# Remainders and 128x1024 products from GpSimd to VectorE in a two-layer decoder trunk, with the loop's weight rows placed anew

## The chip, the cores and the metric

The kernel runs on one core of a Trainium2 chip. The metric is the time of one execution on the device in microseconds (us), the median of several runs. The core's engines are TensorE (matmul; PE in the profile, and PEld for its weight loads), VectorE (DVE), ScalarE (ACT), GpSimd (POOL) and SyncE (SP, which issues the DMAs here).

## The reference

The program computes two layers on x of 1024 tokens by 1024 columns, in float32. Layer 0 is RWKV-7 time mixing, layer 1 differential attention; each ends with a gated embedding, and a root-mean-square norm closes the whole. Layer 0, which most of the change is in, is cut here to what is computed:

```python
dx = token_shift(h) - h                       # h = rms_norm(x)
r, k, v, gate = (h + dx * mu[g]) @ w_in[:, g] # g = 0..3
decay, a = f(h + dx * mu[4]), f2(h + dx * mu[5])
# per head of 64, over the 1024 tokens:
state = state * w_t - (state @ kk_t) * b_t + v_t * k_t
y_t = state @ r_t
y = (y - mean) * rsqrt(var + eps) * ln_w + ln_b
y = y + sum(r * k * r_k) * v                  # bonus
h = x + (y * silu(gate)) @ w_out
h = h + sigmoid(rms_norm(h) @ pe_w_gate) * (p @ pe_w_proj)
```

Layer 1 projects h to q, k, v and a gate for 8 heads, takes softmax twice for each head, subtracts one from the other times lambda, norms, gates, multiplies by w_out, and ends with the same gated embedding.

## The kernel before

**Products in three parts.** A float32 operand is used as two: a high part of reduced precision, which ACT makes by a copy, and the remainder, the operand less its high part. `split` (line 86) issues both; the remainder runs on the engine it is given, on POOL when none is given. A product is then three matmuls (`mm3`, line 90): high by high, high by remainder, remainder by high. So each weight row (128x1024) and each tile of activations needs a remainder before its second matmul.

**Stages in the order of the program.** The norm and the transposes of x; the projections k, r, v and gate, one after another; a loop over 16 chunks of 64 tokens; the gated embedding of layer 0; attention, head by head; its output product and the last gate.

- `make_xm` (line 251) makes the input of projection g for 128 columns and 512 tokens: a scaled copy, a multiply-add on DVE, and a split. `make_half` does eight of them; the halves of v and of gate are made while r and v still run. `wload` (267) loads and splits a weight row: names w1, w0 for k and r, wv for v, w3 for gate.
- Beside v and gate run the inverses of 32x32 blocks (`inv_diag`, 565): sums row by row on DVE (tiles tm and tb), with small products on TensorE before and behind (pb, pg, po).
- In the loop, chunk c has pieces of the chunk itself (`chain_x`, `chain_u`, `chain_s`), of the next chunk's preparation (`stage1`: decayed, turn, mh, pr, bonus), and of the 128-token tile two chunks back (`d1_pieces`: load, norm, squares, bonus_v in the even chunk; sums, roots, scaled, added, turn in the odd one). The tile before that one is multiplied by w_out: m0 (first 512 columns) in the even chunk and m1 in the odd one, in four pieces of two weight rows, which `more` places between the chains. In the first four chunks `more` places products of layer 1's embedding in their stead. `wo_row` (965) splits the rows of w_out, one by one, in chunks 1 to 4.
- `gate_row` (761) makes a gate's weight row, scaled by the norm's vector: with an engine given, ACT scales the row, ACT copies it, and the engine subtracts; with none, ACT writes the scaled high part at once and DVE makes the remainder in one multiply-subtract (`wrow`, 743).

**Order.** In the loop, from line 1091 to 1206, each engine keeps the order in which the program issues its instructions. Elsewhere the framework's planner orders each engine's instructions by its own simulated times; the listing gives only the dependences and priorities. Every engine works through its own queue in order. All DMAs named here are issued on SP's queue, but for the gate's store on ACT's.

Of the kernel before, what the change touches and what calls it, by code (L numbers as in the profile page):

```python
# [16 lines left out]
ALU = mybir.AluOpType  # L17
# [4 lines left out]
P = 128  # L22
D = 1024
SEQ = 1024
KT = D // P
NT = SEQ // P
L = 64
# [10 lines left out]
def trunk(ctx: ExitStack, tc: tile.TileContext, A, out):  # L38
# [47 lines left out]
    def split(hi, lo, src, lo_eng=None):  # L86
        S.activation(hi, src, AF.Copy)
        (lo_eng or G).tensor_tensor(out=lo, in0=src, in1=hi.bitcast(F32), op=ALU.subtract)
# [132 lines left out]
    with NB("ab") as ab, NP("psab") as pp:  # L221
# [29 lines left out]
        def make_xm(g, kt, hf):  # L251
            h, lo = xslot(f"xm{g}_{kt}_{hf}")
            t = ab.tile([P, 512], F32, tag="xmt", name=f"xmt{g}_{kt}_{hf}", bufs=3)
            hc = hT[:, kt, hf * 512 + 1:hf * 512 + 513]
            if kt % 2 and g != 3:
                V.tensor_scalar(out=t, in0=hc, scalar1=cA[:, g, kt:kt + 1], scalar2=None, op0=ALU.mult)
            else:
                S.activation(t, hc, AF.Copy, scale=cA[:, g, kt:kt + 1])
            V.scalar_tensor_tensor(out=t, in0=hT[:, kt, half(hf)], scalar=cB[:, g, kt:kt + 1], in1=t,
                                   op0=ALU.mult, op1=ALU.add)  # L260
            split(h, lo, t, V if kt % (2 if g == 1 else 3 if g != 3 else 8) == 1 else G)
            return h, lo

        def make_half(g, hf):
# [2 lines left out]
        def wload(nm, src):  # L267
            r = wraw(nm + "r")
            nc.sync.dma_start(out=r, in_=src)
            h, lo = wpair(nm)  # L270
            split(h, lo, r)
            return h, lo

        def dense_T(g, src, xm, ev, nxt, tick=lambda: None):
# [581 lines left out]
    with NB("d") as d, NP("psco") as pp:  # L856
# [114 lines left out]
        def d1_pieces(i):  # L971

            w = D1[i]
            rows = slice(i * P, (i + 1) * P)
            y = w["y"]

            def load():
                w["v"] = dt_("vn", f"vn{i}")
                nc.sync.dma_start(out=w["v"], in_=v_d[rows, :])
                w["sg"] = kview(dt_("sg", f"sg{i}"))  # L980
                nc.sync.dma_start(out=w["sg"], in_=sg_d[:, :, rows].rearrange("j p t -> p j t"))
                w["x"] = dt_("xr", f"xr{i}")
                nc.sync.dma_start(out=w["x"], in_=A["x"][rows, :])

            def norm():
                y3 = y.rearrange("p (h l) -> p h l", l=L)
                st = d.tile([P, 4, 16], F32, tag="gst", name=f"gst{i}", bufs=2)
                V.tensor_reduce(out=st[:, 0], in_=y3, axis=AX.X, op=ALU.add)
                V.tensor_scalar(out=st[:, 0], in0=st[:, 0], scalar1=-1.0 / L, scalar2=None, op0=ALU.mult)
                V.tensor_tensor(out=y3, in0=y3, in1=st[:, 0].unsqueeze(2).to_broadcast([P, 16, L]), op=ALU.add)  # L990
                w["st"] = st

            def squares():
                w["sq"] = dt_("sq", f"ysq{i}")
                S.activation(w["sq"], y, AF.Square)

            def bonus_v():
                v3 = w["v"].rearrange("p (h l) -> p h l", l=L)
                G.tensor_tensor(out=v3, in0=v3, in1=bon[:, i].unsqueeze(2).to_broadcast([P, 16, L]), op=ALU.mult)

            def sums():
                st = w["st"]
                V.tensor_reduce(out=st[:, 1], in_=w["sq"].rearrange("p (h l) -> p h l", l=L), axis=AX.X, op=ALU.add)

            def roots():
                st = w["st"]
                mean_eps(st[:, 1], st[:, 1], L, 64e-5)
                rsqrt(st[:, 2], st[:, 1], st[:, 3])

            def scaled():  # L1010
                y3 = y.rearrange("p (h l) -> p h l", l=L)
                V.tensor_tensor(out=y3, in0=y3, in1=w["st"][:, 2].unsqueeze(2).to_broadcast([P, 16, L]), op=ALU.mult)
                G.tensor_tensor(out=y, in0=y, in1=lnw, op=ALU.mult)

            def added():
                V.tensor_tensor(out=y, in0=y, in1=w["v"], op=ALU.add)
                w["gh"] = kview(dt_("gh", f"gh{i}", 2, F32R))
                w["gl"] = kview(dt_("gl", f"gl{i}", 2, F32R))
                w["ps"] = [None, None]

            def turn(hf):
                yg, gh, gl = w["sg"], w["gh"], w["gl"]
                ps = pp.tile([P, 4, P], F32, tag="t", name=f"ytr{i}{hf}", bufs=2)
                hs = slice(hf * 4, hf * 4 + 4)
                for q in range(4):
                    kt = hf * 4 + q
                    T.transpose(ps[:, q], y[:, kt * P:(kt + 1) * P], ident)
                for q in range(4):
                    kt = hf * 4 + q
                    V.scalar_tensor_tensor(out=yg[:, kt], in0=ps[:, q], scalar=vec["ln_b"][:, kt:kt + 1],  # L1030
                                           in1=yg[:, kt], op0=ALU.add, op1=ALU.mult)
                w["sp"] = [(gh[:, hs], gl[:, hs], yg[:, hs])]

            def turned():
                split(*w["sp"].pop(), V)

            def mms(hf, k0):
                gh, gl = w["gh"], w["gl"]
                cs = slice(hf * 512, hf * 512 + 512)
                if k0 == 0:  # L1040
                    w["ps"][hf] = pp.tile([P, 512], F32, tag="mm", name=f"op{i}{hf}", bufs=2)
                for kt in range(k0, k0 + 2):
                    mm3(w["ps"][hf], gh[:, kt], gl[:, kt], wo[kt][0][:, cs], wo[kt][1][:, cs],
                        kt == 0, kt == KT - 1)
                if k0 + 2 == KT:
                    V.tensor_tensor(out=w["x"][:, cs], in0=w["ps"][hf], in1=w["x"][:, cs], op=ALU.add)
                    if hf == 1:
                        nc.sync.dma_start(out=h1_d[rows, :], in_=w["x"])

            def squares1():  # L1050
                sq = dt_("sq", f"h1sq{i}")
                S.activation(sq, w["x"], AF.Square, accum_out=ss1[:, i:i + 1])

            def mk(hf, k0):
                return lambda: mms(hf, k0)

            m0, m1 = [[mk(hf, k0) for k0 in range(0, KT, 2)] for hf in range(2)]
            return dict(load=load, norm=norm, squares=squares, bonus_v=bonus_v, sums=sums, roots=roots, scaled=scaled,
                        added=added, turn=turn, turned=turned, m0=m0, m1=m1, squares1=squares1)

# [19 lines left out]
        def early_row(q):  # L1080
            wg.append(gate_row(0, q, None, EG[q], er[0][:, q], False))

        EG = (G, G)
        TP = {}

        def tile_(i):
# [6 lines left out]
        for c in range(NCH):  # L1093
# [31 lines left out]
                pj["turn"](1)  # L1125
            if w and odd:
                w["roots"]()
            more()
            unit("mh", 0)
            if pj and not odd:  # L1130
# [5 lines left out]
            if c == 2:  # L1136
                wo_row(5)
            if c == 4:
                wo_row(6)
            chain_u(c)  # L1140
            if w:
                w["scaled" if odd else "load"]()
            unit("turn", 0)
            unit("decayed", 1)
            more()
            unit("mh", 1)
            if w and not odd:
                w["norm"]()
            unit("pr", 0, 1)
# [2 lines left out]
                wo_load(4, 5)  # L1152
            if c == 3:
                wo_load(2, 3, 6, 7)
            if c == 4:
                wo_row(7)
            chain_s(c)
            if c == 0:
                wo_load(0, 1)
            if c == 1:  # L1160
                wo_row(4)
            if w and not odd:
                w["squares"]()
                w["bonus_v"]()
# [10 lines left out]
            unit("turn", 1)  # L1175
            if w and odd and c < NCH - 1:
                w["turn"](0)
            more(9)
            unit("bonus", 1)
            if c == 3:  # L1180
                wo_row(2)
                wo_row(3)
            if c == 12:
                early_raw()
            if c == 13:
                early_row(0)
                early_row(1)

        t6, t7 = tile_(NT - 2), tile_(NT - 1)
        m0, m1 = list(t6["m0"]), list(t6["m1"])  # L1190
# [20 lines left out]
        de = ctx.enter_context(NB("de", side="right"))  # L1211
        d2_cm = NB("d2")
        d2 = d2_cm.__enter__()
        GE = (None, None, None, G, None, G, None, G)

        def gate_w():
            kt = len(wg)
# [103 lines left out]
    with tc.tile_pool(name="at", bufs=1, reuse_waits="tile") as at, tc.tile_pool(name="psat", bufs=1, space=PSUM, reuse_waits="tile") as pp:  # L1321
# [226 lines left out]

        wg1 = []

        def gate_pair(kt, tags, eng=G):

            own = None
            if tags == "k1":
                t = at.tile([P, 2, SEQ], F32R, tag="k1", name=f"wg1{kt}", bufs=2)
                own = (t[:, 0], t[:, 1])
            elif tags == "kv":
                own = (at.tile([P, SEQ], F32R, tag="k2", name=f"wg1{kt}h", bufs=2),
                       at.tile([P, SEQ], F32R, tag="vh", name=f"wg1{kt}l", bufs=2))
            elif tags == "q1":  # L1560
                own = (q1[:, 0], q1[:, 1])
            wg1.append(gate_row(1, kt, own, eng))
# [67 lines left out]
            f()  # L1630
        emm(NT - 1, 1)
        for kt in range(4, KT):
            gate_pair(kt, None, G)
        fin = at.tile([P, D], F32, tag="e", name="fin", bufs=3)
        nc.sync.dma_start(out=fin, in_=A["fnorm"].to_broadcast([P, D]))
        nf = [0]
# [113 lines left out]
```

## Time and profile before

| | |
|---|---|
| median of 3 runs | 1774.21 us (1773.93 to 1779.56) |
| profiled execution | 1772.86 us |
| its span, first to last instruction | 1770.7 us |
| TensorE busy | 1674.5 us, 95% |
| DVE, ACT, POOL busy | 72%, 45%, 30% |
| mean granted TensorE clock | 0.964 |
| DMA | 176 MB, mean 99 GB/s |

The span is what the profiler saw of one execution, and the execution's own time is 2.2 us longer. A busy TensorE is not one at its peak: a granted clock below 1 means that the same matmul takes longer. Tile names stand without numbers: xm_1h is the high part of an xm tile of the second half of the tokens, xm_1l its remainder, kbp the output of decayed, pr that of the piece pr, m the masked products of mh, prt the bonus.

### The profile page before, as it was taken

To read this page: it belongs to the slowest core of one execution; us is meant where nothing else is said; L and a number is where in the kernel's file an instruction comes from. 1 tells how busy PE (TensorE), PEld (TensorE's weight loads), DVE (VectorE), ACT (ScalarE), POOL (GpSimd) and SP (SyncE) were. 2 spreads that over 40 slices of the span, in tenths; PEclk is the share of its full clock that TensorE was granted. 3 is DMA by queue.
4 is the path that set the end of the run, shared out by engine and by line. 5 is a ranking of instruction groups with operands and counts; after the bars stand their busy time and mean duration, and the time that the engine had idled before them with its cause. 6 is when DMAs were issued, how large, how long until landed. Compare 5 with 4: busy or idle time off the path is not lost.

```text
span 1770.7 us, 31132 instructions
## 1 busy us (share of the span) xinstructions
PE 1674.5 (95%) x11768; PEld 1393.3 (79%) x11768; DVE 1269.7 (72%) x2940; ACT 797.5 (45%) x1690; POOL 538.8 (30%) x617
## 2 busy tenths in 40 slices
PE   6899999898998999999899999999999999999998
PEld 5677778888677877888678788788888888787786
DVE  7875854697995367765856657887888888856665
ACT  6567843336445343334423433443444444543332
POOL 4533634214413555566400022222222222211200
PEclk9999999998899989998999999999999999999999
DMA  7115444433315654444523410110101101521122
GB/s 264 54 47 174 131 124 109 128 105 93 105 48 162 188 179 126 133 146 136 202 101 126 142 60 7 54 43 22 58 30 34 57 8 57 193 68 35 60 96 72
DMA packets 164404, 176.03 MB, mean 99 GB/s; under 512 B 74845, under 2 KB 127837, under 8 KB 164254
## 3 DMA queue, kind: packets, MB, share of 16 engines
q1 hardware_dynamic: 161950, 169.84, 30.8%
q10 hardware_dynamic: 2304, 4.20, 0.6%
q8 instruction: 93, 1.52, 0.4%
q14 instruction: 57, 0.47, 0.1%
HBM read 124.19 MB, written 49.81 MB: 98 GB/s over the span
## 4 chain that ended last, share of the span: by engine, by line
PE 58%; DVE 26%; issue 5%; ACT 5%; POOL 3%; DMA 3%; SPq 0%; ACTq 0%; DVEq 0%; POOLq 0%
PE qkv L50 15%; PE d L50 6%; PE fg L50 5%; PE do L50 5%; PE pg L50 5%; DVE xmt L50 3%; PE xy L50 3%; DVE tm L50 3%; PE op L50 3%; DVE tb L50 3%; PE sc L50 3%; PE av L50 3%; DVE nb L50 2%; PE pm L50 1%; POOL m L50 1%
## 5 line engine op out<-in xcount | busy, mean ns | idle before, releaser
L50 ACT ACTIVATE e<-sc,mx 128x256 f32<-128x256 f32 (+7 forms) x128 | 94.1, 738 | 106.7 <-DVE mx L50 70.9
L50 POOL TENSOR_TENSOR rp<-rp,rq 128x128 f32<-128x128 f32 x128 | 61.5, 501 | 203.8 <-DVE rq L50 79.0
L50 PE MATMUL sc<-k,q 128*128 128x512 f32 (+2 forms) x384 | 88.8, 362 | 3.3 <-ACT e L50 3.3
L50 PEld LDWEIGHTS av<-vh,aT 128*128 128x128 f32 x576 | 74.7, 191 | 13.1 <-DVE aT L50 4.2
L50 PE MATMUL av<-vh,aT 128*128 128x128 f32 x576 | 78.6, 277 | 5.4 <-ACT o L50 2.9
L50 DVE TENSOR_REDUCE mxs<-sc 128x1 f32<-128x128 f32 (+6 forms) x112 | 73.8, 680 | 0.9
L50 PE MATMUL do<-dwo,oh 128*128 128x512 f32 x224 | 72.3, 404 | 2.2 <-ACT oh L50 1.7
L50 PE MATMUL pg<-pwg,ph 128*128 128x512 f32 x224 | 73.7, 408 | 0.0
L50 POOL CAST q<-q 64x128 fp32r<-64x128 f32 x128 | 38.6, 302 | 113.4 <-PE sc L50 110.1
L50 POOL TENSOR_TENSOR m<-m,mmask 128x512 f32<-128x512 f32 x32 | 47.8, 1494 | 82.1 <-ACT m L50 82.1
L50 PEld LDWEIGHTS sc<-k,q 128*128 128x128 f32 x384 | 63.2, 189 | 12.0 <-ACT e L50 4.4
L50 POOL CAST k<-k 64x256 fp32r<-64x256 f32 x64 | 29.6, 462 | 130.3 <-ACT k L50 99.6
L50 DVE SCALAR_TENSOR_TENSOR xmt<-hT,cB,xmt 128x512 f32<-128x512 f32 x64 | 63.6, 1010 | 6.1 <-ACT xmt L50 5.8
L50 ACT ACTIVATE o<-av,r 128x128 f32<-128x128 f32 x64 | 23.4, 366 | 97.9 <-PE av L50 97.8
L50 DVE TENSOR_TENSOR tm<-tb,nb 128x31 f32<-128x31 f32 (+15 forms) x124 | 56.1, 452 | 3.6
L50 DVE TENSOR_TENSOR rp<-qkv,rc 128x256 f32<-128x256 f32 x64 | 27.0, 421 | 41.9 <-PE qkv L50 36.7
L50 DVE TENSOR_TENSOR tb<-tb,tm 128x31 f32<-128x31 f32 (+15 forms) x124 | 52.8, 426 | 3.6
L50 DVE SCALAR_TENSOR_TENSOR e<-e,r,e 128x128 f32<-128x128 f32 (+3 forms) x64 | 53.8, 841 | 1.2
L50 DVE COPY aT<-at 128x512 f32<-128x512 f32 (+2 forms) x96 | 51.9, 549 | 1.9 <-PE at L50 1.5
L50 DVE TENSOR_TENSOR m<-pm,mmask 128x512 f32<-128x512 f32 x32 | 22.1, 692 | 41.3 <-PE pm L50 41.2
L50 PEld LDWEIGHTS do<-dwo,oh 128*128 128x128 f32 x224 | 41.6, 191 | 11.7 <-ACT oh L50 2.0
L50 PEld LDWEIGHTS pg<-pwg,ph 128*128 128x128 f32 x224 | 42.3, 193 | 9.3 <-ACT ph L50 0.2
(1136 smaller groups left out, 5546.5 us busy)
## 6 DMA issues: line engine op xcount, KB each, us to landing
pp_d<-ppo SPq DMA_DIRECT2D x32, 256.0 KB, 2.3
kb_d<-kb SPq DMA_DIRECT2D x16, 512.0 KB, 3.3
kkr<-kkr_d SPq DMA_DIRECT2D x32, 256.0 KB, 3.5
kb<-kb_d SPq DMA_DIRECT2D x32, 256.0 KB, 3.4
x<-in_x SPq DMA_DIRECT2D x8, 512.0 KB, 4.9
kkr_d<-ep SPq DMA_DIRECT2D x16, 256.0 KB, 2.6
kkr_d<-rt SPq DMA_DIRECT2D x16, 256.0 KB, 2.6
bb<-kb_d SPq DMA_DIRECT2D x32, 128.0 KB, 3.2
```

Source lines behind the costliest of these rows:

```text
L50: r = f(*a, **k)
```

## The change

It moves passes from POOL to DVE, and places some of the loop's pieces elsewhere.

- Remainders of xm for v and gate are all on DVE (before: every third for v, one in eight for gate). Remainders of the weight rows of v and gate are on DVE.
- The bonus product with v (`bonus_v`) and the product of y with ln_w (in `scaled`), both 128x1024, are on DVE.
- Rows 0, 1, 3, 5 and 7 of the first gate and all rows of the last gate take the form without an engine: one ACT pass, one DVE pass.
- In chunk 15 `scaled` and the first gate's row 1 come ahead of the chunk's first products; row 0 stays in chunk 13, a few pieces sooner.
- Tile 0 multiplies w_out's rows in the order 0, 1, 4, 5, 2, 3, 6, 7. Rows 2 and 3 are split in chunk 4 (before: at the end of chunk 3), rows 6 and 7 behind chunk 4's chain_s (before: ahead of it).

```diff
-            split(h, lo, t, V if kt % (2 if g == 1 else 3 if g != 3 else 8) == 1 else G)
+            split(h, lo, t, V if g > 1 or kt % (2 if g == 1 else 3) == 1 else G)
...
-            split(h, lo, r)
+            split(h, lo, r, V if nm[:2] in ("wv", "w3") else G)
...
-                G.tensor_tensor(out=v3, in0=v3, in1=bon[:, i].unsqueeze(2).to_broadcast([P, 16, L]), op=ALU.mult)
+                V.tensor_tensor(out=v3, in0=v3, in1=bon[:, i].unsqueeze(2).to_broadcast([P, 16, L]), op=ALU.mult)
...
-                G.tensor_tensor(out=y, in0=y, in1=lnw, op=ALU.mult)
+                V.tensor_tensor(out=y, in0=y, in1=lnw, op=ALU.mult)
...
+            order = (0, 4, 2, 6) if i == 0 else (0, 2, 4, 6)
...
-            m0, m1 = [[mk(hf, k0) for k0 in range(0, KT, 2)] for hf in range(2)]
+            m0, m1 = [[mk(hf, k0) for k0 in order] for hf in range(2)]
...
-        EG = (G, G)
+        EG = (None, None)
...
+            if c == NCH - 1:
+                w["scaled"]()
+                early_row(1)
             more()
...
             if c == 4:
-                wo_row(6)
+                wo_row(2)
             chain_u(c)
-            if w:
+            if w and c < NCH - 1:
                 w["scaled" if odd else "load"]()
...
             unit("mh", 1)
+            if c == 4:
+                wo_row(3)
...
-            if c == 4:
-                wo_row(7)
             chain_s(c)
...
+            if c == 4:
+                wo_row(6)
+                wo_row(7)
...
+            if c == 13:
+                early_row(0)
             more(9)
             unit("bonus", 1)
-            if c == 3:
-                wo_row(2)
-                wo_row(3)
             if c == 12:
                 early_raw()
-            if c == 13:
-                early_row(0)
-                early_row(1)
...
-        GE = (None, None, None, G, None, G, None, G)
+        GE = (None,) * KT
...
-        def gate_pair(kt, tags, eng=G):
+        def gate_pair(kt, tags, eng=None):
...
-            gate_pair(kt, None, G)
+            gate_pair(kt, None)
```

## Rows read from the trace of the kernel before

**Rows 1.** The page, part 1: busy us (share of span) x instructions.
```profile
PE 1674.5 (95%) x11768; PEld 1393.3 (79%) x11768; DVE 1269.7 (72%) x2940; ACT 797.5 (45%) x1690; POOL 538.8 (30%) x617
```

**Rows 2.** Windows: stretch and its us, engines' busy us, granted clock, DMA share, GB/s.
```profile
300.00:325.00 25.00, 20.10 (x163) 18.38 (x162) 23.84 (x23) 11.57 (x19) 15.95 (x9) 0.99 0.30 74
325.00:562.00 237.00, 220.01 (x2037) 189.93 (x2036) 194.74 (x351) 107.94 (x179) 65.82 (x47) 0.91 0.37 106
562.00:690.00 128.00, 116.78 (x1503) 98.44 (x1502) 72.17 (x101) 51.11 (x89) 66.00 (x51) 0.88 0.53 162
690.00:830.00 140.00, 136.75 (x1997) 117.13 (x1995) 93.31 (x165) 53.94 (x105) 83.66 (x66) 0.97 0.47 145
830.00:905.00 75.00, 64.49 (x510) 51.77 (x509) 50.25 (x94) 31.33 (x44) 29.14 (x16) 0.84 0.48 167
...
1540.00:1680.00 140.00, 134.05 (x657) 109.08 (x657) 90.33 (x238) 55.44 (x107) 20.64 (x14) 0.98 0.22 71
```

**Rows 3.** Timeline, DVE: start, us, engine, line, operation, out<-in [idle before <-releaser].
```profile
316.33 2.77 DVE L50 SCALAR_TENSOR_TENSOR xmt<-hT,cB,xmt 128x512 f32<-128x512 f32 x1
...
365.64 0.39 DVE L50 TENSOR_TENSOR tm<-tb,nb 128x220 f32<-128x220 f32 x1
366.06 2.47 DVE L50 TENSOR_TENSOR tb<-tb,tm 128x220 f32<-128x220 f32 x1
...
533.46 2.42 DVE L50 TENSOR_TENSOR tm<-tb,nb 128x135 f32<-128x135 f32 x1
```

**Rows 4.** Timeline, POOL, beside rows 3.
```profile
365.65 2.63 POOL L50 TENSOR_TENSOR wv21l<-wv21r,wv21h 128x1024 fp32r<-128x1024 f32 x1 [18.82 <-DMA v_d<-vst]
368.23 2.56 POOL L50 TENSOR_TENSOR wv30l<-wv30r,wv30h 128x1024 fp32r<-128x1024 f32 x1
```

**Rows 5.** Timeline, PE, matmuls that came behind a wait.
```profile
324.49 0.52 PE L50 MATMUL v<-wv00h,xm_1h 128*128 128x256 f32 x1 [4.90 <-ACT vst L50]
381.71 2.91 PE L50 MATMUL pg<-prhs,pairs 64*64 64x32 f32 x64 [3.16 <-ACT prhs L50]
481.61 0.47 PE L50 MATMUL pb<-kk,bb 64*64 64x64 f32 x2 [2.32 <-DVE nq L50]
649.78 0.37 PE L50 MATMUL prt<-rk,pr 128*64 128x2 f32 x2 [1.09 <-POOL pr L50]
672.89 0.50 PE L50 MATMUL op<-rwo7l,gh 128*128 128x512 f32 x1 [1.78 <-DVE rwo7l L50]
827.36 0.25 PE L50 MATMUL prt<-rk,pr 128*64 128x2 f32 x2 [0.33 <-ACT kbn L50]
827.92 0.63 PE L50 MATMUL prt<-rk,pr 128*64 128x2 f32 x14 [0.32 <-POOL pr L50]
836.32 0.80 PE L50 MATMUL op<-rwo0h,gl 128*128 128x512 f32 x1 [1.43 <-DVE gl L50]
859.86 1.50 PE L50 MATMUL xy<-vu,m 128*64 128x64 f32 x32 [2.17 <-DVE vu L50]
866.96 0.78 PE L50 MATMUL ytr<-ident,y 128*128 128x128 f32 x4 [2.84 <-DVE y L50]
1661.28 0.56 PE L50 MATMUL o<-ident,o 128*128 128x128 f32 x2 [3.26 <-DVE o L50]
```

**Rows 6.** Timeline, DVE, passes with no POOL row beside them.
```profile
319.02 0.68 DVE L50 TENSOR_TENSOR xm_1l<-xmt,xm_1h 128x512 fp32r<-128x512 f32 x1
...
876.99 1.23 DVE L50 TENSOR_TENSOR y<-y,gst 128x1024 f32<-128x1024 f32 x1
...
878.83 1.28 DVE L50 SCALAR_TENSOR_TENSOR pwg<-pwg06r,vecs,pwg 128x1024 fp32r<-128x1024 f32 x1
```

**Rows 7.** Timeline, ACT, at v's first accumulators.
```profile
323.55 0.63 ACT L50 ACTIVATE xm_1h<-xmt 128x512 fp32r<-128x512 f32 x1 [2.52 <-DVE xmt L50]
```

**Rows 8.** Timeline, POOL, in the loop's odd chunk 9.
```profile
752.53 2.37 POOL L50 TENSOR_TENSOR y<-y,lnw 128x1024 f32<-128x1024 f32 x1 [1.85 <-DVE y L50]
...
755.88 2.27 POOL L50 TENSOR_TENSOR m<-m,mmask 128x512 f32<-128x512 f32 x1
```

More of the change, by code (lines that the diff above doesn't have):

```diff
@@ L1039, in mms @@
                 cs = slice(hf * 512, hf * 512 + 512)
-                if k0 == 0:
+                if k0 == order[0]:
                     w["ps"][hf] = pp.tile([P, 512], F32, tag="mm", name=f"op{i}{hf}", bufs=2)
@@ L1043, in mms @@
                     mm3(w["ps"][hf], gh[:, kt], gl[:, kt], wo[kt][0][:, cs], wo[kt][1][:, cs],
-                        kt == 0, kt == KT - 1)
-                if k0 + 2 == KT:
+                        kt == order[0], kt == order[-1] + 1)
+                if k0 == order[-1]:
                     V.tensor_tensor(out=w["x"][:, cs], in0=w["ps"][hf], in1=w["x"][:, cs], op=ALU.add)
```

## The prediction

> **What bounds the kernel now.** I read the page's busy row, then busy time and clock by stage, the timelines of DVE, POOL and ACT, TensorE's waits, and the loop's POOL queue. TensorE is busy 95% of the span [rows 1], so a change can give back only two things: time in which TensorE idles, and time in which the granted clock is at the lower of its two levels (1.2 instead of 2.4 GHz). The windows give both for a stage: its length less PE busy, and its length times one less the granted clock [rows 2].
>
> - 300 to 325 us (r's stage turns into v's): 4.9 idle, 0.3 for the clock.
> - 325 to 562 (v and gate projections, the 32x32 inverses beside them): 17.0 idle, 0.09 x 237 = 21.3 for the clock; 38 together.
> - 562 to 690 (chunks 0 to 5): 11.2 and 15.4.
> - 690 to 830 (chunks 6 to 13): 3.3 and 4.2.
> - 830 to 905 (end of the loop, first gate rows): 10.5 and 12.0.
> - 1540 to 1680 (attention's end): 6.0 and 2.8.
>
> The rest issues no operation that the diff touches. The low clock follows the waits: the stages with long waits have 0.84 to 0.91, those without have 0.97 and more; the short stage of the first point has its low stretch only behind its end [rows 2].
>
> Why TensorE waits is in the next views. A DVE product of two SBUF tiles that starts while a POOL product runs does not slow a little, it stands until POOL is done: the inverse's 128x220 rows take 0.39 us, the one that starts at 366.06 takes 2.47 and ends within 0.2 us of the POOL row that ran from 365.65 [rows 3, 4]. Nine DVE rows between 366 and 534 are like this (the first and the last stand in the group), each about 2.07 over its neighbours: 18.7 us. TensorE's waits for the inverse come behind them: 3.16 at 381.71 and 2.32 at 481.61 [rows 5]. DVE is busy 194.7 of 237 there [rows 2], so it is near its own bound.
>
> A rule of the Trainium skill speaks against the change (Perfetto Trace Analysis, Optimizing Scalar/DVE Operations): as DVE and GpSimd share a read port, moving work between them might not help. By that the sum would keep only what the changed order gives; it is a rival below.
>
> **Part by part.** All sums are against the profiled execution, 1772.86 us (span 1770.7 and 2.2 around it); the median of the three runs is 1774.21, 1.35 higher.
>
> A moved 128x1024 pass costs POOL 2.4 to 2.6 [rows 4, 8]; on DVE a product of two SBUF tiles of that size takes 1.23, one with a scale 1.28, and a 128x512 remainder 0.68 [rows 6]. So a move halves the time for which the pair is held, but it puts on DVE what POOL could do beside DVE's transposes and PSUM reads, where nothing was blocked.
>
> *r to v, 300 to 325.* TensorE's 4.90 wait at 324.49 is for the ACT copy that empties v's first accumulator [rows 5]; that copy is queued behind the activation of the last xm row (323.55), which waited 2.52 for DVE [rows 7]. Off POOL go five remainders of v's second half and two weight rows. DVE gets 5 x 0.65 + 2 x 1.2 = 5.7 of work, and loses eight blocked rows (xm rows of 128x512; the worst took 2.77 [rows 3]), about 9.6 over. Net 3.7 off the wait, and a little of the low clock after it: **-4**. Bounds: 0 (the planner puts the weight rows ahead of the xm rows) and -6.6 (the wait and 1.7 of clock).
>
> *v and gate, 325 to 562.* Thirteen weight remainders come to DVE, 13 x 1.15 = 15.0 (1.23 with the overlap of neighbours off), against 18.7 blocked: -3.7. The fourteen gate remainders (0.68 each, 9.5) take away as many POOL passes of 128x512 that stand beside DVE's xm rows; I put them at even. So DVE is hardly relieved; what goes is that the inverse stands still for 2 us at a time behind work of which its place in the order takes no account. The order here is the planner's, not the program's, and it will see these passes on DVE. I take a quarter of the 38 us: **-10**. Bounds: +9 (the weight remainders fall on the inverse's chain and the blocked rows go only in part: 15 + 9.5 less 18.7, and two low stretches of 1.7 each) and -25 (two thirds of the 38, which DVE's 42 free us allow).
>
> *Chunks 2 to 5.* The bonus product leaves POOL, so norm's y at chunk 2 isn't blocked and the state is earlier. At chunk 3 y's scaling no longer stands ahead of kbp, m and pr on POOL, where the bonus matmuls waited 1.09 and more [rows 5]; DVE does it in 1.2, but copy, mask, state and sum stand behind it there, so the transposes of y come no sooner; of 3 us some 1.2 go, and the next chunk starts 2.4 earlier. Weight rows 2 and 3, now in chunk 4, take the old places of 6 and 7; 6 and 7 go behind chain_s, with the state ahead of them on DVE and y's two copies ahead on ACT. Their products are last in the new order (0, 4, 2, 6) but TensorE is there at 670.3, row 7's remainder at about 675.2 (state at 672.9, then two rows of 1.2): the 1.78 wait [rows 5] becomes 4.3. The bonus product then waits behind both rows, and the next chunk's sums behind it. -1.1 - 2.4 + 2.5, and some clock: **-3**. Bounds +4 and -9.
>
> *Chunks 6 to 13.* Per odd chunk POOL does y (2.37), kbp, m (2.27), pr, and the bonus matmuls wait for pr: 0.33 for POOL and 0.33 just before it [rows 8, 5]. Without y on POOL pr is 2 to 4 us earlier, and both small waits go: five chunks, 3.3; the low stretches in this window are worth 4.2 more [rows 2]. What DVE gets: 1.23 between y's scaling and the mask of the odd chunk, which is for the next chunk's unit; 1.23 between state and residual of the even one, ahead of sums and roots. The mask and state rows move back by at most that, and TensorE wants them 4 us later; where that cover is gone, a chunk costs 1.2. **-6**. Bounds +3 and -7.5.
>
> *830 to 905.* Early row 0 as one scaled ACT pass and one DVE row, instead of two ACT passes and a POOL row each: the 1.43 wait for gl goes, with 0.66 at 827.92. Row 1 stands ahead of chunk 15's first products; DVE does y, its scaling and that row (1.2 + 1.2 + 1.3 behind the roots at 853.7) and comes to vu at 857.3, against 858.4: the 2.17 wait at 859.86 is 1.0. y's sum then needs no POOL: the 2.84 at 866.96 goes. Rows 3, 5 and 7 give one DVE row each and one ACT pass less. 5.4 of waits and half of the 12 of clock: **-11**. Bounds -3 and -18.
>
> *Attention's end.* Rows 4 to 7 of the last gate go to DVE; the norm's small DVE rows ahead of the 3.26 wait at 1661.28 [rows 5] are blocked by two POOL remainders today. Up to two rows of 1.28 can stand there instead: **-3**. Bounds 0 and -5.
>
> Sum: 4 + 10 + 3 + 6 + 11 + 3 = 37 off 1772.86: 1736; with the 1.35, **1737 us** against 1774.21. All the gains at their bound give 1703, all the losses 1787.
>
> **Rivals.**
> - *DVE becomes the bound of v and gate.* The 24.5 us come on top, the blocked time doesn't go (what blocks is something else than the remainders), and the inverse ends 24 later, at 567; the loop's first loads need its tiles. For: DVE is busy 82% of the stage. Against: the ends of blocked DVE rows coincide with POOL's [rows 3, 4]. +24, +6 for the clock, less half of the last three parts (10) and -3, -4: about 1787. It decides when less than some 10 of the 18.7 are given back.
> - *No gain from the move itself* (a pass holds the same pair wherever it runs, and DVE gives back in its queue what it saved in blocking); only the order's parts remain, chunks 2 to 13 and the end of the loop at half: 3 + 6 + 5.5: 1760. The Trainium skill's sentence above is this rival; the trace's 1.23 against 2.37 bears it out only in part.
> - *The waits go, the low clock stays* (the loop's small matmuls, not the waits, bring it): 3.7 + 5 + 1 + 3.3 + 5.4 + 2.5 = 21: 1753.
> - *The planner follows and nearly all waits of v and gate go:* -25 there, -18 at 830 to 905, the rest as forecast: 1715.
> - *It cancels:* chunk 4's longer wait and +9 in v and gate eat the loop's gain; within 5 us of 1774.
>
> **Chances.** Forecast 0.38 (1725 to 1746), no gain from the move 0.19, clock stays 0.13, planner 0.15, cancel 0.07, DVE bound 0.08. The last but one is "same", the last "slower"; 0.3% of 1774 is 5.3 us, about what a measurement can tell from no change. Faster 0.85, same 0.07, slower 0.08. The range that leaves out 2 in 10 reaches from the planner's case to the upper side of "no gain": 1711 to 1767.
>
> **What would show it.** Right: no DVE row of the inverse above 1 us between 366 and 534 but beside POOL's memsets; the wait for vst under 2 us; granted clock 0.94 or more in v and gate; no wait of the bonus matmuls in odd chunks; a longer wait for a weight row in chunk 4; no 2.84 before y's transposes. Wrong: the inverse's last transpose later than now against the stage's start, or mask and state rows in the loop for which TensorE waits.

## The result

The changed kernel takes 1756.45 us (median of four runs, 1754.39 to 1758.03), the kernel before 1774.07 (1773.35 to 1779.56): a ratio of 0.9888, 95% interval 0.9868 to 0.9907, so 17.6 us faster. Forecast were 1737, 37 faster. The sign is right and the time lies in the range of 1711 to 1767, but outside the forecast's own 1725 to 1746: less than half of the gain came. The two profiled executions are 1772.86 and 1757.43, 15.4 apart; what follows splits these.

The page's busy row after, against [rows 1]:

```profile
PE 1665.5 (95%) x11768; PEld 1384.7 (79%) x11768; DVE 1268.1 (72%) x3009; ACT 786.1 (45%) x1677; POOL 407.4 (23%) x548
```

POOL lost 131.4 us of work, 69 more DVE instructions run, and yet DVE is busy 1.6 less. What DVE took over is about what it had spent standing still before. TensorE's time outside work went from 96.2 to 90.1 (span less busy), the share lost to the clock from 0.036 to 0.032 of the span, 63.7 to 56.2 us.

The start of the first TensorE row of each stage, in the profiled executions, and the change of its length against the forecast (the boundaries are the program's, so they move with the kernel; pg is the first gate's product, qkv and do are attention's first and last products):

```
stage                              before            after       length   forecast
start to chunk 0                0.0 - 574.7     0.0 - 555.1      -19.6    -4 -10
chunks 0, 1                   574.7 - 613.8   555.1 - 596.1       +2.0      0
chunks 2 to 5                 613.8 - 691.8   596.1 - 673.1       -1.0     -3
chunks 6 to 13                691.8 - 828.5   673.1 - 806.1       -3.7     -6
chunks 14, 15, to first pg    828.5 - 887.0   806.1 - 861.5       -3.1    -11
first gate                    887.0 - 1002.8  861.5 - 979.0       +1.7      0
attention (qkv to do)        1002.8 - 1537.7  979.0 - 1522.0      +8.2      0
do to last gate's products   1537.7 - 1667.3 1522.0 - 1652.0      +0.4     -3
last gate                    1667.3 - 1770.7 1652.0 - 1755.6      +0.2      0
```

More than forecast came before the loop (19.6 for 14), little at the loop's end, and 8 were lost in attention, of which the diff touches no operation.

The windows after, for the stretches that answer [rows 2] (busy of PE, PEld, DVE, ACT, POOL; granted clock; DMA share; GB/s):

```profile
300.00:325.00 25.00, 25.00 (x225) 22.77 (x224) 19.62 (x34) 12.93 (x21) 0.00 (x0) 1.00 0.44 114
325.00:542.00 217.00, 205.88 (x1987) 179.24 (x1985) 190.65 (x379) 105.17 (x172) 14.42 (x20) 0.95 0.36 104
542.00:670.00 128.00, 115.13 (x1489) 96.14 (x1486) 69.11 (x101) 53.26 (x91) 58.85 (x49) 0.85 0.57 170
670.00:805.00 135.00, 133.68 (x1966) 114.35 (x1964) 96.87 (x170) 52.32 (x101) 73.28 (x58) 0.99 0.51 152
805.00:880.00 75.00, 61.85 (x543) 49.55 (x542) 53.04 (x106) 26.99 (x42) 7.61 (x7) 0.91 0.51 168
1525.00:1665.00 140.00, 134.04 (x656) 108.56 (x655) 92.75 (x245) 50.12 (x104) 2.02 (x5) 0.98 0.21 70
```

In the first, TensorE has no idle left and the full clock: the idle of r's turn into v, 4.9 before, is gone, as forecast. In v and gate the clock is 0.95 for 0.91. The fifth has 13.2 idle, more than the 10.5 before.

DVE, the inverse of v's stage, answering [rows 3] (start, us, engine, line, operation, out<-in):

```profile
362.70 1.23 DVE L50 TENSOR_TENSOR wv30l<-wv30r,wv30h 128x1024 fp32r<-128x1024 f32 x1
363.84 0.38 DVE L50 TENSOR_TENSOR tm<-tb,nb 128x220 f32<-128x220 f32 x1
364.81 0.38 DVE L50 TENSOR_TENSOR tb<-tb,tm 128x220 f32<-128x220 f32 x1
```

A weight remainder costs 1.23 and the row behind it 0.38. The 248 rows of the inverse take 84.7 us together where they took 108.9, and none is over 1 us where 14 were. Nine of the 14 are the prediction's; the other five, of 1.38 to 1.51, stood beside POOL's remainders of gate's xm rows. One of them, before:

```profile
462.69 1.48 DVE L50 TENSOR_TENSOR tm<-tb,nb 128x240 f32<-128x240 f32 x1
```

TensorE's waits after, answering [rows 5] (the wait and its releaser in brackets):

```profile
645.43 0.50 PE L50 MATMUL op<-rwo6h,gh 128*128 128x512 f32 x1 [0.65 <-ACT rwo6h L50]
647.99 0.50 PE L50 MATMUL op<-rwo6l,gh 128*128 128x512 f32 x1 [2.06 <-DVE rwo6l L50]
649.08 0.49 PE L50 MATMUL op<-rwo7h,gh 128*128 128x512 f32 x1 [0.36 <-ACT rwo7h L50]
650.34 0.79 PE L50 MATMUL op<-rwo7l,gh 128*128 128x512 f32 x1 [0.77 <-DVE rwo7l L50]
672.52 0.63 PE L50 MATMUL prt<-rk,pr 128*64 128x2 f32 x16 [0.33 <-ACT kbn L50]
834.24 1.97 PE L50 MATMUL xy<-vu,m 128*64 128x64 f32 x32 [4.65 <-DVE vu L50]
838.34 0.60 PE L50 MATMUL ytr<-ident,y 128*128 128x128 f32 x4
843.70 0.50 PE L50 MATMUL op<-rwo0h,gh 128*128 128x512 f32 x1 [2.92 <-ACT gh L50]
860.13 1.09 PE L50 MATMUL ptr<-ident,n 128*128 128x128 f32 x8 [2.99 <-DVE n L50]
1645.77 0.56 PE L50 MATMUL o<-ident,o 128*128 128x128 f32 x2 [2.32 <-DVE o L50]
```

The longer wait for the weight rows in chunk 4 is there (0.65 + 2.06 + 0.36 + 0.77 = 3.84), in odd chunks POOL's half of the bonus wait is gone and ACT's 0.33 stays, and y's transposes wait no more. Longer is the wait in chunk 15 for vu, the input of the chunk's second products: 4.65 for 2.17. New is the 2.92 for gh, the high part of the gated tile that w_out multiplies. DVE's queue ahead of vu:

```profile
828.07 1.23 DVE L50 TENSOR_TENSOR y<-y,lnw 128x1024 f32<-128x1024 f32 x1
829.22 1.28 DVE L50 SCALAR_TENSOR_TENSOR pwg<-pwg0raw,vecs,pwg 128x1024 fp32r<-128x1024 f32 x1
830.41 1.28 DVE L50 SCALAR_TENSOR_TENSOR pwg<-pwg04r,vecs,pwg 128x1024 fp32r<-128x1024 f32 x1
831.61 1.28 DVE L50 SCALAR_TENSOR_TENSOR pwg<-pwg05r,vecs,pwg 128x1024 fp32r<-128x1024 f32 x1
832.80 1.38 DVE L50 TENSOR_TENSOR vu<-u,rn 64x512 f32<-64x512 f32 x2
```

Ahead of vu stands not one gate row but three: rows 4 and 5 are outside the stretch with the written order, and the planner sets them in where its simulated times leave room. Row 4 stood there before too, and DVE idled 3.37 for ACT's pass of it:

```profile
857.22 1.28 DVE L50 SCALAR_TENSOR_TENSOR pwg<-pwg04r,vecs,pwg 128x1024 fp32r<-128x1024 f32 x1 [3.37 <-ACT pwg L50]
```

On ACT row 2 now stands ahead of gh and waits for its own load:

```profile
841.98 1.15 ACT L50 ACTIVATE pwg<-pwg02r,vecs 128x1024 fp32r<-128x1024 f32 x1 [4.55 <-DMA pwg02r<-in_pwg]
```

Attention's first 127 us, before and after (windows):

```profile
1002.80:1062.00 59.20, 57.91 (x271) 47.06 (x270) 35.56 (x96) 22.70 (x64) 14.81 (x34) 1.00 0.25 80
1062.00:1130.00 68.00, 64.88 (x351) 54.56 (x350) 54.26 (x175) 30.82 (x92) 14.52 (x40) 1.00 0.11 38
```

```profile
979.00:1038.00 59.00, 54.94 (x247) 43.96 (x246) 31.18 (x84) 20.15 (x57) 11.98 (x29) 0.97 0.20 62
1038.00:1106.00 68.00, 64.63 (x341) 54.34 (x340) 55.15 (x175) 31.21 (x92) 15.57 (x42) 0.98 0.14 44
```

In the same time TensorE issues 24 and 10 matmuls fewer. It idles 4.1 instead of 1.3 in the first window, and by the rounded clock 1.8 and 1.4 more are lost to its lower level. The built order differs there too: before, the first qkt transposes stand in the fifth qkv tile, after, behind it.

### The profile page after: what moved, and what is told of

It is laid out like the page before. It is cut to its first block, busy times and chain, and to the rows that moved or that the text cites. A ratio compares the mean times of both kernels' runs of the same rounds, so it can differ in the third digit from the quotient of the medians.

```text
span 1755.6 us, 31089 instructions
## 1 busy us (share of the span) xinstructions
PE 1665.5 (95%) x11768; PEld 1384.7 (79%) x11768; DVE 1268.1 (72%) x3009; ACT 786.1 (45%) x1677; POOL 407.4 (23%) x548
## 4 chain that ended last, share of the span: by engine, by line
PE 72%; DVE 16%; DMA 4%; ACT 4%; issue 3%; SPq 0%; POOL 0%; ACTq 0%; DVEq 0%
PE qkv L50 17%; PE d L50 10%; PE fg L50 5%; PE op L50 5%; PE do L50 5%; PE pg L50 5%; PE xy L50 3%; PE sc L50 3%; PE v L50 3%; PE av L50 3%; DVE xmt L50 2%; PE pm L50 2%; DVE nb L50 1%; PE pps L50 1%; PE at L50 1%
## 5 line engine op out<-in xcount | busy, mean ns | idle before, releaser
L50 POOL TENSOR_TENSOR m<-m,mmask 128x512 f32<-128x512 f32 x32 | 43.2, 1352 | 108.2 <-ACT m L50 108.2
L50 POOL CAST q<-q 64x128 fp32r<-64x128 f32 x128 | 39.1, 306 | 108.9 <-PE sc L50 105.5
L50 DVE SCALAR_TENSOR_TENSOR xmt<-hT,cB,xmt 128x512 f32<-128x512 f32 x64 | 57.0, 906 | 0.9 <-ACT xmt L50 0.7
L50 POOL MEMSET tb<- 128x1024 f32 (+1 forms) x8 | 4.5, 560 | 213.2 <-DVE ti L50 201.2
L50 PEld LDWEIGHTS do<-dwo,oh 128*128 128x128 f32 x224 | 41.4, 190 | 11.6 <-ACT oh L50 2.1
L50 ACT ACTIVATE k<-qkt 64x256 fp32r<-64x256 f32 x64 | 24.0, 375 | 55.4 <-DVE k L50 27.5
```

Source lines behind the costliest of these rows:

```text
L50: r = f(*a, **k)
```

## The experiments

Each stage start below is that of the profiled execution; in the eight kernels with both remainders of v and gate on DVE and nothing on POOL beside them chunk 0 starts at 553.1 to 556.4. Medians are of four to ten runs, ratios against the kernel before in the same session. In the diffs `...` marks what is left out.

**Which part gains?** Three kernels with one part each.

```diff
 vg_only, against before
-split(h, lo, t, V if kt % (2 if g == 1 else 3 if g != 3 else 8) == 1 else G)
+split(h, lo, t, V if g > 1 or kt % (2 if g == 1 else 3) == 1 else G)
...
-split(h, lo, r)
+split(h, lo, r, V if nm[:2] in ("wv", "w3") else G)
 loop_only: the changed kernel without these two, and with
+GE = (None, None, None, G, None, G, None, G)
...
+def gate_pair(kt, tags, eng=G):
...
 gates_only, against before
+GE = (None,) * KT
...
+def gate_pair(kt, tags, eng=None):
...
```

> Only the remainders of v's and gate's xm rows and of v's and gate's weight rows are on DVE; the loop and the gate rows are as before. Theory (the gain is made between 300 us and the loop, and the planner's other order in attention takes 8 back): chunk 0's first products at 555 +-3 instead of 574.7, the loop as long as before, attention's heads 8 longer: 1763 (1758 to 1768). Rival (the loop's edits bring the gain, v and gate give back before the loop what they save): chunk 0 at 570 or later, 1774 or more. Rival (no gain from the move itself): DVE's rows of the inverse over 1 us as often as before, 1774.

> Only what stands inside the loop is changed: bonus product, y's scaling, order of the weight rows and of the first tile's products, the two early gate rows and chunk 15's order; v, gate, the later gate rows and the last gate as before. Theory: chunk 0 at 574.7 +-1.5 as before; chunks 2 to 14 give 8 to 10, chunk 15 to the first gate products lose 2 to 3 of it, attention's heads are 8 longer by the planner's order: 1776 (1772 to 1780). Rival (my forecast for the loop and its end, 3 + 6 + 11): 1754 to 1760.

> Only the gate rows (three of the first gate, all of the last) give their remainder to DVE in one pass; all else as before. The built order of attention's first head is then that of the changed kernel. Theory (the order of that head costs 5 and two later head boundaries 3): the span from the first qkv product to the first do product is 543 instead of 534.8, the rest within 3: 1781 (1777 to 1784). Rival (attention's loss comes from what the earlier stages leave behind, such as late loads, and not from its order): 535, and 1771 to 1774.

```
             chunk 0  chunk 6  chunk 14  first pg  first qkv  qkv to do   median  ratio (95%)
before         574.7    691.8     828.5     887.0     1002.8      534.9
vg_only        554.0    671.2     807.9     866.2      980.7      538.3   1762.50  0.9922 (0.9894 to 0.9950)
loop_only      576.6    695.9     827.3     880.6      996.9      541.6   1774.39  0.9996 (0.9979 to 1.0013)
gates_only     576.9    689.8     829.6     888.2     1006.2      539.6   1780.55  1.0035 (1.0017 to 1.0054)
```

The remainders of v and gate alone bring chunk 0 20.7 forward, and the loop keeps these 20.7 to the first gate product. The loop's own part is worth about 8 from chunk 0 to there (312.3 before, 304.0; all of it ahead of chunk 15), and all of it is given back, most of it behind, where attention is 6.7 longer. The gate rows alone make the kernel slower: attention is longer by 4.7, not by the 8 that I expected of its order alone. (vg_only's profiled execution, 1755.86, was the shortest of its five; by the medians the gain of the remainders is 10.5.)

**Is it POOL beside DVE?** The gain of vg_only, with POOL's work put back as rows that nobody reads.

```diff
 pool_filler, against vg_only
...
+if nm[:2] in ("wv", "w3") and nm not in ("w3_6", "w3_7"):
...
+    for o, n in ((0, 384), (384, 384), (768, 256)):
+        G.tensor_tensor(out=dummy[:, 0:n], in0=r[:, o:o + n], in1=h[:, o:o + n].bitcast(F32), op=ALU.subtract)
```

> The kernel with only v's and gate's remainders on DVE, and beside them 14 of the 16 weight rows get a second remainder on POOL in three pieces (384, 384 and 256 columns), whose result nobody reads; TensorE's, DVE's and ACT's order stays the same but for a few places around gate's first xm rows. DVE has the work of the changed kernel, POOL nearly that of the kernel before. Theory (a POOL product holds up DVE's products of two SBUF tiles, and that is what v and gate gained): DVE rows of the inverse over 1 us are back, and chunk 0 comes 8 to 20 later than the 554 without the filler: 1770 to 1782. Rival (the gain is the shorter way, one engine less, or the planner's order, and POOL's rows beside DVE cost nothing): chunk 0 at 554 +-2, 1762.

Measured: 1774.14, ratio 0.9998 (0.9980 to 1.0017). Chunk 0 starts at 570.5, 16.5 later than without the filler; this execution was the longest of ten and vg_only's the shortest of five, and the medians are 11.6 apart. Nine rows of the inverse are over 1 us again, none in vg_only. DVE of this kernel, and POOL beside it:

```profile
365.31 0.40 DVE L50 TENSOR_TENSOR tm<-tb,nb 128x231 f32<-128x231 f32 x1
365.62 1.22 DVE L50 TENSOR_TENSOR wv21l<-wv21r,wv21h 128x1024 fp32r<-128x1024 f32 x1
366.76 1.21 DVE L50 TENSOR_TENSOR tb<-tb,tm 128x231 f32<-128x231 f32 x1
367.89 2.03 DVE L50 TENSOR_TENSOR wv30l<-wv30r,wv30h 128x1024 fp32r<-128x1024 f32 x1
369.84 0.92 DVE L50 TENSOR_TENSOR tm<-tb,nb 128x220 f32<-128x220 f32 x1
```

```profile
365.70 4.81 POOL L50 TENSOR_TENSOR dummy<-wv21r,wv21h 128x384 f32<-128x384 f32 x3 [19.41 <-DMA v_d<-vst]
```

The order of the queues is nearly the same, and each DVE product now stands behind a piece of POOL's, as POOL's three pieces stand behind DVE's (4.81; elsewhere in this run, where DVE leaves them room, three take 2.9). So most of what v and gate had lost was due to POOL's products beside DVE's; vg_only also has another built order there than before, and whether that gives the 4.2 that the filler does not take back is open. That a DVE operation with two SBUF inputs and a POOL operation that reads SBUF exclude each other is stated by the Trainium skill (SBUF — State Buffer, Who interferes with whom); these rows agree: DVE's row at 366.76 takes 1.21, the like one at 365.31, free of POOL, 0.40.

**Weight rows or xm rows?** vg_only in its two halves: w_only has only its second line, xm_only only its first.

> Only the weight rows' remainders of v and gate are on DVE, the xm rows as before. By my forecast the weight rows carry v's and gate's gain (18.7 blocked against 15.0 of work, and the inverse no longer stands), while the xm rows are even but for 4 at v's start: chunk 0 at 558 to 564 instead of 574.7 (554 with both): 1764 to 1772. Rival (the xm rows carry it, as each of them blocked DVE too): chunk 0 at 568 to 574, and 1775 to 1782 with attention's other order.

> Only the remainders of v's and gate's xm rows are on DVE; their weight rows stay on POOL. The weight rows alone brought chunk 0 from 574.7 to 567.9, both parts to 554. Theory (what counts is whether any POOL product stands beside DVE's; so neither part brings its share alone, and with the weight rows left on POOL the inverse is still held up): chunk 0 at 564 to 570, 1766 to 1774. Rival (the parts add: the xm rows bring the other 14): chunk 0 at 560 to 562, 1760 to 1765.

Measured: w_only chunk 0 at 567.9, 1771.00, ratio 0.9982 (0.9962 to 1.0002); xm_only 565.5, 1771.98, ratio 0.9974 (0.9955 to 0.9992). The weight rows are not the larger part, as I had it: 6.9 and 9.3 of 20.7, and 4.6 only with both (of single executions, w_only's the longest of its ten). The inverse rows over 1 us number 14 before, 7, 8, and 0 with both.

**The weight rows' new places.**

```diff
 rows_undone, against the changed kernel
-order = (0, 4, 2, 6) if i == 0 else (0, 2, 4, 6)
+order = (0, 2, 4, 6)
...
 chunk 3: wo_row(2), wo_row(3) at its end; chunk 4: wo_row(6) ahead of chain_u, wo_row(7) ahead of chain_s, as before
```

> The changed kernel with the weight rows 2, 3, 6 and 7 at their old places and the first tile's products in the old order (0, 2, 4, 6). From chunk 2's start to chunk 6's took 77.9 before and 76.9 in the changed kernel. Theory (the new places only move the wait from chunk 3 to chunks 4 and 5, what chunk 3 gained came half from y's scaling): 75 to 77, and 1753 to 1757. Rival (the new places pay): 79 to 81, and 1758 to 1761.

Measured: 1742.67, ratio 0.9830 (0.9796 to 0.9864). Chunks 2 to 5 take 71.3; I had 75 to 77 for my theory. Windows of that stretch, rows_undone and then the changed kernel:

```profile
593.70:665.00 71.30, 67.18 (x964) 56.90 (x962) 52.60 (x85) 29.35 (x52) 33.10 (x28) 0.93 0.53 163
```

```profile
596.10:673.10 77.00, 69.64 (x966) 58.11 (x964) 52.49 (x85) 29.52 (x52) 34.53 (x28) 0.91 0.50 151
```

The same matmuls, 3.2 less idle and a higher clock. Behind the waits of chunk 4 the changed kernel's clock is at its lower level; in rows_undone it is not (the changed kernel, then rows_undone):

```profile
650.00:660.20 10.20, 9.87 (x89) 8.74 (x90) 5.34 (x16) 3.12 (x6) 1.05 (x1) 0.50 0.18 52
```

```profile
640.00:665.00 25.00, 23.23 (x350) 19.32 (x346) 21.32 (x37) 9.36 (x16) 13.09 (x12) 1.00 0.35 98
```

Over all runs with the loop's edits the four kernels with the new places need 76.9, 78.5, 78.6 and 80.6 for chunks 2 to 5, the four with the old ones 68.2, 69.8, 69.8 and 71.3: the new places cost some 9. TensorE idles 6.7 to 7.4 there with the new places and 4.1 to 4.2 with the old, and 6.8 to 11.9 against 1.7 to 5.1 are lost to the clock. Of the rest of the 13.8, 3 lie between chunk 14 and the first gate product, where the planner set row 5 behind vu, and 1.6 in chunk 8, where a low stretch (a time at the lower clock) is missing.

**The loop's end.** Orders held by dependencies that need no semaphore. `fence` keeps an instruction to stand behind: S is ACT's copy to the second gh, V the second vu; n is the normed tile of the first gate, ph and pl the high part and the remainder of its transposes.

```diff
 c15_fix, against the changed kernel (turns() fixes an order on one engine)
+if nm in ("pwg02", "pwg03"):  turns([fence["S"], a])   # ACT pass behind the second gh of tile 6
+if nm in ("pwg04", "pwg05"):  turns([fence["V"], b])   # DVE pass behind chunk 15's vu
...
 end_held: c15_fix with rows_undone, and
+if nm in ("pwg06", "pwg07"):  turns([fence["n" if nm == "pwg06" else "pl"], b])
 end_ph: end_held, and
+if nm in ("pwg06", "pwg07"):  turns([fence["ph"], a])   # ACT pass behind the second ph
```

> The changed kernel with two orders held: gate rows 4 and 5 give their DVE pass behind chunk 15's vu, and gate rows 2 and 3 their ACT pass behind the second gh of tile 6. Theory (the end of the loop lost its gain because the gate rows, once on DVE and ACT alone, stood ahead of vu and gh): the 4.65 wait for vu becomes 2.1 to 2.5, the 2.92 wait for gh under 1, one or two low stretches of 3.41 go: from chunk 15's start to the first gate product 32 to 35 instead of 39.2, and 1750 (1747 to 1754). Rival (vu waits for y's own two passes and early row 1, and gh for the transposes, so these rows do not matter): both waits as before, 38 to 40, 1756 or more.

Measured: 1746.66, ratio 0.9853 (0.9821 to 0.9885). From chunk 15 to the first gate product 35.5 instead of 39.2, 3.7 where I expected 4 to 7; the whole time is just below the range that I gave. TensorE, then DVE:

```profile
831.50 1.15 PE L50 MATMUL xy<-vu,m 128*64 128x64 f32 x32 [1.56 <-DVE vu L50]
836.97 0.50 PE L50 MATMUL op<-rwo0h,gh 128*128 128x512 f32 x1 [0.47 <-ACT gh L50]
856.26 1.97 PE L50 MATMUL ptr<-ident,n 128*128 128x128 f32 x8 [7.84 <-DVE n L50]
```

```profile
853.41 1.28 DVE L50 SCALAR_TENSOR_TENSOR pwg<-pwg06r,vecs,pwg 128x1024 fp32r<-128x1024 f32 x1 [3.85 <-ACT pwg L50]
```

Both waits went (4.65 to 1.56, 2.92 to 0.47), and 4.85 came back at the next join (the next place where TensorE needs another engine's result): DVE stood at row 6, whose load was not in, with the last step of the norm's root and n behind it. The same mechanism, one place on. So rows 6 and 7 were held too.

> The changed kernel with the weight rows at their old places and the order at the loop's end held: gate rows 4 and 5 behind vu on DVE, rows 2 and 3 behind the second gh on ACT, row 6 behind the first point's n and row 7 behind its pl on DVE. With row 7 there the planner gives TensorE in attention the very order of the kernel before. Theory (each gate row ahead of vu, gh or n on its queue costs what it takes or waits for its load, and attention's other order costs 3 to 5): from chunk 15's start to the first gate product 29 to 32 (34.7 with the rows' old places alone), attention 534 to 536 from first qkv to first do product: 1735 (1731 to 1739). Rival (the wait ends at the next join whatever stands in the queues, as 2.99 became 7.84 when vu and gh were early): 34 or more, 1738 to 1743.

Measured: 1731.60, ratio 0.9751 (0.9727 to 0.9775). To the first gate product 33.0 (I had 29 to 32; the rows' old places alone, in rows_undone, give 34.7), attention 537.1 (534 to 536). The wait for n is 2.18, and the join behind it has the rest, as ACT stands at row 6. TensorE and ACT:

```profile
838.70 1.09 PE L50 MATMUL ptr<-ident,n 128*128 128x128 f32 x8 [2.18 <-DVE n L50]
843.64 1.22 PE L50 MATMUL pg<-pwg,ph 128*128 128x512 f32 x2 [3.84 <-ACT ph L50]
```

```profile
840.70 1.15 ACT L50 ACTIVATE pwg<-pwg06r,vecs 128x1024 fp32r<-128x1024 f32 x1 [6.98 <-DMA pwg06r<-in_pwg]
```

> As end_held, and gate rows 6 and 7 also give their ACT pass behind the second ph of the first point. In end_held ACT stood 6.98 at row 6 until its load was in, with ph behind it, and TensorE waited 3.84 for ph. Theory (a gate row at the head of a queue passes the wait for its own load on to whatever stands behind it): that wait falls under 1, chunk 15's start to the first gate product is 29 to 30.5 instead of 33; TensorE then waits at most 1.5 for rows 6 and 7 inside the first gate product: 1728 (1725 to 1731). Rival (rows 6 and 7 are then late by as much, as their loads are what is late): the sum of the waits from chunk 15 to the second gate product stays within 1 of end_held's, and 1731 to 1733.

Measured: 1730.30, ratio 0.9755 (0.9737 to 0.9774); to the first gate product 29.4.

```profile
841.39 1.09 PE L50 MATMUL ptr<-ident,n 128*128 128x128 f32 x8 [2.19 <-DVE n L50]
842.73 1.22 PE L50 MATMUL pg<-pwg,ph 128*128 128x512 f32 x2 [0.25 <-ACT ph L50]
844.41 0.80 PE L50 MATMUL pg<-pwg,pl 128*128 128x512 f32 x1 [0.46 <-DVE pl L50]
```

The wait did not come back further on: the rows were not late, they stood too early. The totals of end_ph and end_held do not differ beyond their intervals; the profiled execution of end_ph came 2.7 later to chunk 15, for a cause that stays open. These two are the fastest versions, 24 to 26 us under the changed kernel.

**Attention.** Two tests of its order.

```diff
 att_order, against the changed kernel: TensorE's order held
+if h == 0 and i == 3 and kt == 0:  turns([htr[-5], ms[1]])     # the last pair's third transposes ahead of tile 3
...
+if h == 0 and i == 4 and kt == 1:  turns([qk[0, 0], ms[0]])    # qkt of tiles 0, 1 ahead of the rest of tile 4
 end_held_row7, against end_held
-turns([fence["n" if nm == "pwg06" else "pl"], b])
+turns([fence["n"], b])
```

> The changed kernel, with TensorE's order at attention's start held near that of before: the last pair's transposes and the first two qkt transposes stand ahead of the rest of the fourth and fifth qkv tile. Theory (that order is what costs): head 0 gets back 3 to 5, the later boundaries perhaps 3: 1751 (1747 to 1754). Rival (TensorE then waits at those transposes for DVE and ACT rows whose order is still the new one): 1756 or more.

> As end_held, but row 7's DVE pass stands behind n (ahead of pl) instead of behind pl. That alone turns the planner's order in attention to the changed kernel's. Theory (that order costs, not the change's remainders): attention 538 to 541 from first qkv to first do product instead of 534 to 536; the end of the loop within 1.5 of end_held; 1739 (1735 to 1743), 3 to 5 over end_held. Rival (attention's loss is chance of the run, low stretches that come and go): both kernels within 1.5.

att_order: 1753.52, ratio 0.9871 (0.9841 to 0.9900), within the interval of the changed kernel's. The time lies in the theory's range, but the stage does not bear it out: attention takes 538.1, 4.9 less than in the changed kernel's profile, and 3.4 of that is the clock, which did not fall there in this execution. Head 0 got back less than 1 beside the clock: TensorE waited 1.64 at the held transposes for DVE's rows, which kept much of their new order, as the rival had it. end_held_row7: 1737.61, ratio 0.9783 (0.9759 to 0.9808), 6.0 over end_held, and all its runs lie above all of end_held's; attention 542.0 against 537.1. (The profiled executions are 9.6 apart; of the rest 2.3 lie before chunk 0 and 2.2 behind attention.) Here the queues of all engines changed together, by the place of one gate row 130 us earlier. Over all runs, kernels with attention's other order take 538.1 to 543.0 from qkv to do (ten profiles, mean 540.6), those with the order of before 534.9, 537.1 and 537.1. TensorE idles 9.6 to 10.3 there in these three and 12.2 to 14.2 in the ten, and the clock takes 0 to 1.7 and 0 to 3.4. So the order costs some 4, and single executions with it differ by up to 5, in part by the clock; of the 8.2 in the changed kernel's profile 4.4 are idle and 3.4 the clock.

## Why the prediction was right or wrong

The direction was right, and so was what brings it: DVE hardly stands behind POOL any more. Of the six signs of being right five came; the sixth, no wait of the bonus matmuls in odd chunks, came by half.

*r to v, -4: right.* The wait of 4.90 is gone, the clock full in the window.

*v and gate, -10: the mechanism right, the size too small.* 19.6 less 5 for r's end is 14.6. The mis-sized term is "I put them at even" for the gate's xm remainders: DVE lost 28 us of blocked time between 325 and chunk 0 (29.4 to 1.4, each row's duration over that of its kind unblocked), not 18.7. I had counted only the nine rows of the inverse beside weight rows; five more stood beside xm rows (462.69 above), and xm rows were blocked by xm rows too. My reading that the weight rows carry the gain fell with w_only and xm_only.

*Chunks 2 to 5, -3: the sum near (-1.0), two terms wrong, so by luck.* "-1.1 - 2.4 + 2.5": y's scaling and the bonus product on DVE are worth some 8 (78.0 to a mean of 69.8 with the old places), the new places cost some 9. The longer wait was foreseen (4.3, measured 3.84); what was left out is the clock: behind the four short waits (rwo6h to rwo7l) it stands at its lower level for 10.2 us, and in all four kernels with the new places it takes more than in the four with the old ones.

*Chunks 6 to 13, -6: the mechanism right, -3.7 here and -5.3 in others.* 131.4 in five kernels with the loop's edits and 133.0 in three, the changed one among them, against 136.7 to 143.0 in six without them (136.7 before). Only half of the bonus wait went: the 0.33 for kbn is ACT's, and I had booked it to POOL.

*830 to 905, -11: wrong; the step that failed.* It says that DVE "comes to vu at 857.3, against 858.4", after y, its scaling and row 1: 1.1 sooner. Measured from chunk 15's start vu comes 10.6 after it, against 8.1 before: 2.5 later. The step counted what the program writes ahead of vu, not what the planner puts there: rows 4 and 5, 1.28 each, and on ACT row 2 with 4.55 of waiting for its load. Row 4 at 857.22 in the trace of before, with its wait of 3.37, could have warned: the 858.4 is where vu stood behind that row. From chunk 14 to the first gate product it takes 58.5 before, 55.4 changed, 51.7 with rows 2 to 5 held (c15_fix), and 45.6 with all of them held (end_ph), 13 less than before. Of the way from 55.4, 3 come with the weight rows' old places (rows_undone, 52.4), where the planner set row 5 behind vu unasked.

*Attention's end, -3: wrong.* The 3.26 became 2.32, and the clock still drops behind it; do to the last gate's products is as long as before (128.3 to 132.3 over all kernels). The blocked rows of the norm (ost) were there and are gone, but two gate rows took their place in the queue, as the prediction allowed, and only 0.94 was left of its 3. DVE before and after:

```profile
1655.19 2.26 DVE L50 TENSOR_TENSOR ost<-ost 128x2 f32<-128x2 f32 x1
1657.49 2.47 DVE L50 SCALAR_TENSOR_TENSOR ost<-ost 128x2 f32<-128x2 f32 x2
```

```profile
1640.49 1.28 DVE L50 SCALAR_TENSOR_TENSOR pwg<-pwg14r,vecs,pwg 128x1024 fp32r<-128x1024 f32 x1
1641.76 1.28 DVE L50 SCALAR_TENSOR_TENSOR pwg<-pwg15r,vecs,pwg 128x1024 fp32r<-128x1024 f32 x1
```

*Not in the sum: attention, +8.* "The rest issues no operation that the diff touches" is true and was taken for "the rest takes as long". Outside the pinned stretch the planner orders anew.

*The rivals.* The time lies between "no gain from the move itself" (1760) and "the waits go, the low clock stays" (1753), some 3.5 from each, and by chance. The first had v and gate unchanged, and they gave most: vg_only has chunk 0 20.7 sooner, and pool_filler's rows on POOL take 16.5 of it away. The rule behind it, that moving work between DVE and GpSimd might not help as they share a read port (the Trainium skill, Perfetto Trace Analysis, Optimizing Scalar/DVE Operations), is not borne out here. The second had the clock unchanged, and about half of the gain is the clock: 7.5 (63.7 to 56.2), against 6.1 of idle. A total alone would have confirmed a wrong rival; the split by stage tells them apart.

## What to carry to other kernels

Where two engines exclude each other, sum the blocked time of every row on the busier one, not of the long rows alone: each row's time over its own unblocked duration came to 29.4 us here, and the move took nearly all of it away. That is not the gain one for one: DVE got new work for it, and the stage came 14.6 sooner. Where a planner orders the queues, a pass that changes engines must be looked for ahead of the join that it could delay, and a row whose load may be late never belongs at the head of a queue that the critical chain shares: hold it behind the join, and follow the wait to the next join until it is gone (39.2, 35.5, 33.0, 29.4 from chunk 15 to the first gate product; the third and fourth also have the weight rows' old places, which alone give 34.7). A change is not local under a planner: compare the order of all stages, and judge parts by their stage, not by the total.

## What the runs showed that I had not expected

- One gate row's place on DVE turns the planner's order of attention 130 us later, at 4.9 us between qkv and do.
- The blocking is mutual: three POOL pieces of 128x384 and less take 2.9 together where DVE leaves them room and 4.81 beside two DVE remainders.
- The two halves of the move bring chunk 0 6.9 and 9.3 forward alone and 20.7 together, in single executions.
